# Multi-query attention on one core: a planner's times for GpSimd's loads, key copies and additions, and a fifth buffer for VectorE's weights

## The chip, the core and the metric

The kernel runs on one core of a Trainium2 chip. The metric is the device time of one execution in microseconds (us); below 2% two kernels of this case can hardly be told apart. TensorE (PE) multiplies matrices, VectorE (DVE), ScalarE (ACT) and GpSimd (POOL) work elementwise, SyncE (SP) issues DMAs. Each engine works through its own instructions in order, so a wait at the head holds all that is behind it.

## What is computed

Attention with 16 heads of queries and one head of keys and values, for 8 batches, 1024 positions and a head dimension of 64, float32 in and out:

```python
scores = np.matmul(q, k.transpose(0, 1, 3, 2)) / np.sqrt(head_dim)
weights = np.exp(scores - np.max(scores, axis=-1, keepdims=True))
weights = weights / np.sum(weights, axis=-1, keepdims=True)
attn_out = np.matmul(weights, v)
```

## The kernel before

**Tiles.** The work is 64 pairs of heads (8 batches by 8 pairs). A pair has 8 tiles of 128 keys, a tile two halves of 512 queries, so there are 1024 score tiles of 128 keys by 2 heads by 512 queries. A score is two matmuls of TensorE into one of three PSUM buffers (`score`, L574). It is then turned into weights, in one of two ways:

- ScalarE takes most scores: one exponential each (`exp_act`, L594), into `wt`, which has 20 buffers (ABUFS).
- VectorE takes a fifth of them, two tiles (four scores) at a time, called a duo, into `wd` with 4 buffers (DBUFS). It writes the scaled score as a 16-bit integer (`fixed`, L602), whose upper bits are already the exponent, and corrects it with a polynomial of the lower bits: `f` (L620), `m` (L623), `l` (L646, done by GpSimd in four parts), the product `m` (L631) and two products into `l` (L633). The correction is added to `wd` by a DMA that accumulates, issued from GpSimd (`add`, L658), two for each duo. In the first duo and the last two VectorE does `l` (L627) and the addition (L637) itself.

The weights are then multiplied with the values (`value`, L683: TensorE, 65 columns, of which the last sums the weights), seven blocks of 128 queries of a head at a time into one of two accumulators. VectorE takes the reciprocal of the sum (L692) and normalises into `osb` (L702), which holds the results of three pairs, and SyncE writes them out (L719). There are 8192 matmuls of L683 and 2048 of L574.

**Transfers.** Keys, values and queries are loaded by GpSimd's DMAs, which cast to float16. Queries come in groups of four pairs, in four parts (`load_part`, L503), with four buffers `qn`; SyncE issues for each part a DMA that transposes it into `qt` (`trans_q`, L512). Keys come batch by batch (`load_k`, L443); GpSimd copies one tile of them behind the others (`copy_k`, L457), and two transposing DMAs of SyncE make `k2t` (`trans_k`, L465). Transposes wait for the exponential before the last one planned and for the last addition (`after`); in the kernel before every addition waits for such an exponential too (L662).

**The order** on all five engines is written out by `plan`. It plays the work through with a cost for each step and emits the steps in order of its own time: the program then has that order, whatever the chip does. `transfers` gives for each load, key copy and transpose the progress in pairs at which it falls due. `issue` hands them to GpSimd and SyncE. In it an addition is ready ADD_0 + ADD_1 + ADD_L after its issue for TensorE (`ready`), transposes and additions are held apart by `hold`, a query load needs a free buffer (`free_q`), and a query transpose is planned LOAD_L after its load. A key copy has no such time: it is planned where it falls due, whether or not the load has landed. LEAD is how many pairs VectorE's scores may run ahead of ScalarE's. At each step TensorE takes a score for ScalarE, a score for VectorE or a block of values, by what the plan's model has ready.

Of the kernel before, what the change touches and what calls it, by code (L numbers as in the profile page):

```python
# [10 lines left out]
FP16 = mybir.dt.float16  # L11
# [6 lines left out]
P = 128  # L18
# [9 lines left out]
VEC_DEP = 0.12  # L28
POOL_S, POOL_F, POOL_L = 0.15, 1.05, 0.12
POOL_D = dict(add=1.0, loadq=0.85, loadk=0.85, copyk=0.95, loadv=1.2)  # L30
ADD_0, ADD_1, ADD_L = 2.0, 2.5, 3.5
TURN_0, TURN_1, LOAD_L = 1.0, 4.0, 6.0
NB, NG, OSB = 16, 7, 3
PITCH = 68
FIRST, DVE_0 = 4, 2.3
ABUFS, DBUFS = 20, 4
LAG, END = 1.0, 6.0
LEAD, LEAD_0, LEAD_END = 2.5, 1.5, 10.0
FIRST_Q, FIRST_G = 3.5, 22.0
QLEAD = 3.3  # L40
LATE = 2
# [4 lines left out]
FAR = 1e9  # L46
# [25 lines left out]
def transfers(NP):  # L72
    QP, HP = 4, 8
    res = []
    for g in range(1, NP // QP):
        for i in range(QP):
            at = QP * (g - 2) + i + 0.2 if g > 2 else 1.2 + 0.8 * i if g > 1 else 0.02 + 0.01 * i
            res += [(at, "loadq", g, i), (at + (0.5 if g > 1 else 0.0), "turnq", g, i)]
    for b in range(1, NP // HP):
        at = HP * (b - 1)  # L80
        res += [(at + 1.5, "loadk", b), (at + 2.2, "copyk", b), (at + 2.5, "turnk", b, 0),
                (at + 3.5, "turnk", b, 1), (at + 2.9, "loadv", b)]
    return sorted(res)


def plan(NP, NKT, stats=None):
# [3 lines left out]
    def emit(t, *op):  # L90
        ops.append((t, len(ops), op))

    def half(t):
# [4 lines left out]
        if i % 2 == 1:  # L98
            avail[d, i // 2] = pool + POOL_L

    def issue(t):
        nonlocal pool, sp, busy, hold, free_q
        while todo_d and todo_d[0][0] <= prog:
            x = todo_d.pop(0)[1:]
            (turns if x[0][:4] == "turn" else loads).append(x)
        if turns and t >= max(sp, busy - TURN_0):
            x = turns[0]
            at = landed.get(x[1:3] if x[0] == "turnq" else x[1:2], FAR)
            if at <= t:
                turns.pop(0)  # L110
                emit(t, *x)
                free_q += x[0] == "turnq"
                sp = t + TURN_0
                hold = t + TURN_1
        if pool > t or halves and zs:
            return
        if adds and adds[0][0] <= t and t >= hold - ADD_0:
            _, d, h = adds.pop(0)
            emit(t, "add", d, h)
            pool = t + POOL_D["add"]  # L120
            busy = max(busy, t + ADD_0) + ADD_1
            ready[duos[d][h]] = busy + ADD_L
        elif loads and not adds and (loads[0][0] != "loadq" or free_q > 0):
            x = loads.pop(0)
            free_q -= x[0] == "loadq"
            emit(t, *x)
            pool = t + POOL_D[x[0]]
            if x[0] in ("loadq", "copyk"):
                landed[x[1:]] = pool + (LOAD_L if x[0] == "loadq" else 0.0)

    pe = act = 0.0
    dve = DVE_0
# [22 lines left out]
    direct: set = set()  # L155
    pool = lock = sp = busy = hold = prog = 0.0
    todo_d = transfers(NP)
    free_q = 4
    adds: list = []
    loads: list = []  # L160
    turns: list = []
# [4 lines left out]
    while todo_g or groups:  # L166
        if pe <= dve:
            T = pe
            prog = ap + (na / nap if ap >= 0 else 0)
            issue(T)  # L170
            if not vunits and not over:
                lead = min(LEAD if prog > 4 else LEAD_0, LEAD * (NP - prog) / LEAD_END) if duos else 0
# [8 lines left out]
                if okay and prog < NP - STOP:  # L181
# [3 lines left out]
                    d = len(duos)  # L185
# [39 lines left out]
            for grp in groups:  # L225
                k, segs, left, a = grp
                for n, j in sorted(left):
                    gp, lo, hi = segs[n]
                    t = NKT * gp + j
                    if t in owner:  # L230
                        r = ready.get(t, FAR)
                    else:
                        r = max(
                            ready.get((t, c), FAR) for c in range(2)
                            if lo < NB // 2 + NB // 2 * c and hi > NB // 2 * c
                        )
                    if len(left) == NKT * len(segs):
                        r = max(r, acc[a])
# [6 lines left out]
            if av:  # L245
                x = pick[0][1][pick[1]]
                after = aa + AV_B * (x[2] - x[1]) + SWITCH
            if kind == "z":
                do = "qk"
            elif kind == "act":  # L250
                s = min(range(3), key=lambda s: slot[s])
                at = aq if slot[s] <= aq else slot[s] + WAKE
# [10 lines left out]
            if do == "qk":  # L263
                s = min(range(3), key=lambda s: slot[s])
                st = aq if slot[s] <= aq else slot[s] + WAKE
                pe, mode = st + QK_P, "qk"
                if kind == "z":
                    d, i = vunits.pop(0)
# [14 lines left out]
            elif do == "av":  # L283
                st = aa
# [10 lines left out]
                if not left:  # L295
                    acc[a] = FAR
                    r = pe - AV_B + PE_R
# [5 lines left out]
        else:  # L303
            T = dve
            issue(T)
            z = [x for x in zs if x[0] <= T]
            todo = [("ev", x) for x in evs if x[0] <= T and (
                x[4] == "rec" or x[:4] + ("rec",) not in evs)]
            if steps:
                x = steps[0]  # L310
# [6 lines left out]
            what, x = (free or todo or [("", None)])[0]  # L317
            if z:
                x = z[0]
# [15 lines left out]
            elif what == "ev":  # L335
                evs.remove(x)
                _, k, segs, a, kind = x
# [42 lines left out]
def kernel(  # L380
# [8 lines left out]
    B, S, H, D = q.shape  # L389
    assert D == 64 and S == 1024 and H % 4 == 0  # L390
    NKT = S // P
# [4 lines left out]
    QP = HP // 2  # L396
# [5 lines left out]
    consts = ctx.enter_context(tc.tile_pool(name="consts", bufs=1))  # L402
# [12 lines left out]
    osb = osbp.tile([P, OSB * NB, D], FP32, name="osb")  # L415
# [15 lines left out]
    def after(i, xs):  # L431
        for x in xs:
            tc.add_manual_dep(
                i.ins, x.ins.name,
                mybir.DependencyInfo(mybir.DependencyClass.Sync, mybir.DependencyReason.DATA),
                reason="transposes and additions apart",
            )
# [43 lines left out]
    def place_q(g):  # L481


        qt[g] = qtp.tile([P, QP * NKT + 1, P], FP16, tag="qt", name=f"qt{g}")[:, 0 : QP * NKT, :]
# [4 lines left out]
    def load_q(p):  # L489

        qn[0, p] = qp.tile([P, NKT, P], FP16, tag="qn", name=f"qn0_{p}")
        if p > 0:
            nc.gpsimd.dma_start(
                out=qn[0, p],
                in_=q[0, :, 2 * p : 2 * p + 2, :].rearrange("(c p) h d -> p c (h d)", p=P),
            )
# [29 lines left out]
    def load_first():  # L526

        st = kst.setdefault(0, {})
        st["kn"] = osb[:, 0:NKT, :]
        st["qf"] = osb[:, NB : 2 * NB, :].rearrange("p (c h) d -> p c (h d)", h=2)  # L530
        for c in range(NQC):
            x = slice(HT * c, HT * c + HT)
            nc.sync.dma_start(
                out=st["kn"][:, x, :], in_=k[0].rearrange("(p c) d -> p c d", p=P)[:, x, :])
            nc.scalar.dma_start(
                out=st["qf"][:, x, :],
                in_=q[0, :, 0:2, :].rearrange("(c p) h d -> p c (h d)", p=P)[:, x, :],
            )
        st["k16"] = consts.tile([P, NKT, 2, D], FP16, name="k160")
        st["k2t"] = kvp.tile([P, NKT + 1, P], FP16, tag="k2t", name="k2t0")[:, 0:NKT, :]  # L540
        place_q(0)
        load_q(0)
# [64 lines left out]
    def flat(x):  # L607
        return x.rearrange("p t h x -> p (t h x)")
# [44 lines left out]
            reason="VectorE reads PSUM next",  # L653
        )

    def add(d, h):
        x = slice(h * 2 * S, (h + 1) * 2 * S)
        added.append(nc.gpsimd.dma_start(  # L658
            out=flat(wd[d].bitcast(I16))[:, x], in_=tmp[d, "l"].bitcast(I16)[:, x],
            accum_op=ALU.add,  # L660
        ))
        after(added[-1], past[-2:-1])  # L662

    def value(k, seg, j, first, s):

# [28 lines left out]
    def normalise(k, segs):  # L694
# [14 lines left out]
        for p, lo, hi in segs:  # L709
# [8 lines left out]
            elif p < NP - 1 and left[p] == 0:  # L718
                nc.sync.dma_start(out=o, in_=x)  # L719

    ops, duos = plan(NP, NKT)
    ops = [op for _, _, op in ops]
    groups = grouped(NP)
    lasts = {}
    for op, *args in ops:
        if op == "av":
            lasts[args[0], args[1][0]] = args[2]
    load_first()
    load_q(1)
    load_v(0)  # L730
# [9 lines left out]
    with tc.manual_schedule(engines={ENG.PE, ENG.Activation, ENG.DVE, ENG.Pool, ENG.SP}):  # L740
# [4 lines left out]
        for op, *args in ops:  # L745
            if op == "qk":
# [3 lines left out]
                t, c, s = args  # L750
                if t in units:
                    d, i = units[t]
# [5 lines left out]
            elif op == "z":  # L758
                d, i = args
                fixed(duos[d][i // 2], i % 2)  # L760
            elif op == "step":
                poly(*args)
            elif op == "l":
                linear(*args)
            elif op == "add":
                add(*args)
            elif op == "av":
                value(*args)
            elif op == "rec":
                reciprocal(*args)  # L770
            elif op == "norm":
                normalise(*args)
            elif op == "loadq":
                load_part(*args)
            elif op == "turnq":
                trans_q(*args)
            elif op == "loadk":
                load_k(*args)
            elif op == "copyk":
                copy_k(*args)  # L780
            elif op == "turnk":
                trans_k(*args)
            elif op == "loadv":
                load_v(*args)
            else:
                raise ValueError(op)
# [28 lines left out]
```

## Time and profile before

| what | value |
|---|---|
| runs shown | 768.44, 773.98, 779.84 us; median 773.98 |
| profiled execution | 771.87 us, its span 770.0 us |
| mean granted clock of TensorE | 0.970 |
| busy in the span | ScalarE 746.5 us, VectorE 730.2, TensorE 686.7, GpSimd 394.4 |
| first and last exponential | start at 6.98 us, end at 758.82 us |
| additions, issue to landing | 6.7 us at the median, 102 of 512 KB |

In a row of groups, the numbers behind the first bar are the busy time in us and the mean duration of one in ns; behind the second bar is the idle time of the engine before them, with what ended it. A row of waits has the total in us, how often, and the longest. A row of the timeline has the start, the time that the row covers, the instruction, how many, and in brackets the idle time before it and what ended it. A row of sums by stretch of time has the busy time of TensorE's matmuls, of its weight loads, of VectorE, ScalarE and GpSimd with the number of instructions in brackets, then the granted clock of TensorE (1.00 is full), the busy share of the DMA engines and GB/s. TensorE's busy time is modelled at the ends of its matmuls.

### The profile page before, as it was taken

The numbers are of one execution on the slowest core, as the hardware profiler recorded it, in microseconds if no ns is written. First come the engines' busy times: TensorE is split into PE (matmuls) and PEld (weight loads), VectorE is DVE, ScalarE is ACT, GpSimd is POOL, SyncE is SP. The second block draws the span as 40 slices with busy tenths as digits, with TensorE's granted clock in tenths as the row PEclk, the third lists the DMA queues.
The fourth block names the chain that finished last, engine by engine and source line by source line (L and its number), as shares of the span: only waits on it lengthen the run. The fifth ranks groups of instructions, "written<-read, shape, count | busy, mean of one in ns | idle before, by whom it ended". The sixth has DMA issues, their size and how long they took to land.

```text
span 770.0 us, 23649 instructions
## 1 busy us (share of the span) xinstructions
PE 686.7 (89%) x10256; PEld 416.8 (54%) x10256; DVE 730.2 (95%) x815; ACT 746.5 (97%) x811; POOL 394.4 (51%) x405
## 2 busy tenths in 40 slices
PE   5888999998999799999989998979889998999985
PEld 2455565655555355555556555545555555556544
DVE  5999998999999879999999999989999999999997
ACT  7999999999999999999999999989999999999994
POOL 3256455555556544565656654655564646444410
PEclk8899999999999979999999999999999999999988
DMA  9789889998999997999989999999999998967443
GB/s 171 119 134 188 158 180 176 184 186 164 182 186 143 164 164 154 196 167 199 177 152 182 178 188 143 184 172 169 191 158 178 170 193 151 187 135 151 87 111 84
DMA packets 185624, 126.18 MB, mean 164 GB/s; under 512 B 89392, under 2 KB 172464, under 8 KB 185520
## 3 DMA queue, kind: packets, MB, share of 16 engines
q0 software_dynamic: 43456, 71.97, 57.0%
q1 hardware_dynamic: 140480, 51.92, 33.6%
q8 instruction: 80, 1.31, 0.7%
q10 hardware_dynamic: 1584, 0.79, 0.4%
q14 instruction: 24, 0.20, 0.1%
HBM read 37.75 MB, written 33.55 MB: 93 GB/s over the span
## 4 chain that ended last, share of the span: by engine, by line
ACT 62%; PE 12%; DVE 12%; issue 7%; DMA 6%; POOL 1%; POOLq 0%; DVEq 0%; ACTq 0%
ACT wt L594 61%; PE sc L574 6%; PE acc L683 5%; DMA wd<-l 4%; DVE wd L602 3%; DVE l L633 2%; DVE m L631 2%; DVE osb L702 1%; DVE m L623 1%; DMA k<-in_k_dram 1%; DVE f L620 1%; DMA k2t<-k 1%; POOL l L646 1%; DMA osb<-in_q_dram 0%; DVE wd L637 0%
## 5 line engine op out<-in xcount | busy, mean ns | idle before, releaser
L594 ACT ACTIVATE wt<-sc 128x1024 f16<-128x1024 f32 x808 | 744.0, 1196 | 8.5 <-PE sc L574 8.1
L574 PE MATMUL sc<-qt,k2t 64*128 64x512 f16 x2048 | 378.9, 392 | 66.7 <-ACT wt L594 52.0
L646 POOL TENSOR_SCALAR l<-f 128x1024 f16<-128x1024 uint16 x204 | 214.0, 1049 | 222.4 <-DVE m L631 111.4
L683 PE MATMUL acc<-v,wt 128*128 128x65 f16 x6464 | 316.9, 195 | 2.3 <-DVE osb L702 2.0
L683 PEld LDWEIGHTS <-wt 128*128 128x128 f16 x6464 | 239.5, 98 | 146.5 <-issue 145.3
L602 DVE TENSOR_SCALAR wd<-sc 128x1024 uint16<-128x1024 f32 x216 | 262.7, 1216 | 17.5 <-PE sc L574 16.6
L574 PEld LDWEIGHTS <-k2t 64*128 64x128 f16 x2048 | 123.3, 93 | 148.6 <-issue 98.9
L658 POOL DMA_DIRECT2D wd<-l x102 | 103.1, 1028 | 88.6 <-ACT wt L594 46.2
L633 DVE TENSOR_TENSOR l<-m,l 128x2048 int16<-128x2048 f16 x108 | 129.6, 1201 | 6.9 <-POOL l L646 6.6
L631 DVE TENSOR_TENSOR m<-f,m 128x4096 f16<-128x4096 uint16 x54 | 123.7, 2291 | 0.1
L683 PE MATMUL acc<-v,wd 128*128 128x65 f16 x1728 | 104.0, 195 | 3.8 <-DMA wd<-l 2.2
L683 PEld LDWEIGHTS <-wd 128*128 128x128 f16 x1728 | 71.7, 98 | 46.4 <-issue 40.2
L702 DVE TENSOR_TENSOR osb<-acc,rec 128x448 f32<-128x448 f32 (+4 forms) x165 | 91.0, 563 | 1.9 <-DVE rec L692 0.2
L623 DVE TENSOR_SCALAR m<-f 128x4096 f16<-128x4096 uint16 x54 | 69.4, 1285 | 0.3
L620 DVE TENSOR_SCALAR f<-wd 128x4096 uint16<-128x4096 uint16 x54 | 64.9, 1202 | 0.0
L503 POOL DMA_DIRECT2D qn<-in_q_dram x60 | 55.3, 922 | 18.7 <-DMA qt<-qn 8.5
L692 DVE RECIPROCAL rec<-acc 128x7 f32<-128x7 f32 (+1 forms) x147 | 27.9, 193 | 2.6 <-PE acc L683 2.2
L451 POOL DMA_DIRECT2D v<-in_v_dram x8 | 10.1, 1264 | 0.0
L457 POOL COPY k<-k 128x64 f16<-128x64 f16 x7 | 4.4, 635 | 8.6 <-DMA k<-in_k_dram 8.3
L637 DVE TENSOR_TENSOR wd<-wd,l 128x2048 uint16<-128x2048 uint16 x6 | 7.2, 1214 | 0.0
L443 POOL DMA_DIRECT2D k<-in_k_dram x7 | 5.7, 811 | 0.4
L560 PE MATMUL kps<-ident,k 128*128 128x128 f16 x8 | 1.2, 307 | 4.1 <-DVE k L548 4.1
(19 smaller groups left out, 19.4 us busy)
## 6 DMA issues: line engine op xcount, KB each, us to landing
wd<-l POOLq DMA_DIRECT2D x102, 512.0 KB, 6.7
out_dram<-osb SPq DMA_DIRECT2D x63, 512.0 KB, 6.2
qn<-in_q_dram POOLq DMA_DIRECT2D x63, 256.0 KB, 6.5
v<-in_v_dram POOLq DMA_DIRECT2D x8, 128.0 KB, 7.5
qt<-qn SPq DMA_TRANSPOSE x63, 4.2
k<-in_k_dram POOLq DMA_DIRECT2D x7, 128.0 KB, 6.8
osb<-in_q_dram ACTq DMA_DIRECT2D x2, 256.0 KB, 4.0
osb<-in_k_dram SPq DMA_DIRECT2D x2, 128.0 KB, 3.2
```

The lines of the kernel that those rows point to most:

```text
L503: nc.gpsimd.dma_start(out=qn[g, i], in_=q[b, :, 2 * QP * r : 2 * QP * (r + 1), :].rearrange("(c p) h d -> p c (h d)", p=P)[:, n * i : n * ...
L574: nc.tensor.matmul(sc[t, c][:, h, :].rearrange("p (i x) -> p i x", x=P), keys(p // HP, h, j), queries(p, c)[64 * h : 64 * h + 64, :, :], s ...
L594: past.append(nc.scalar.activation(out=wt[t][:, :, c * QC : (c + 1) * QC], in_=sc.pop((t, c)), func=EXP, scale=ascale))
L602: behind["dve"] = nc.vector.tensor_scalar(out=wt[t].bitcast(U16)[:, :, c * QC : (c + 1) * QC], in0=sc.pop((t, c)), scalar1=vscale, scalar2 ...
L620: i = V.tensor_scalar(out=new(d, "f", U16, 1), in0=z, scalar1=1023, scalar2=None, op0=ALU.bitwise_and)
L623: i = V.tensor_scalar(out=new(d, "m", FP16, 1), in0=tmp[d, "f"], scalar1=-ONE, scalar2=1.0 / ONE, op0=ALU.add, op1=ALU.mult)
L631: i = V.tensor_tensor(out=tmp[d, "m"], in0=tmp[d, "f"], in1=tmp[d, "m"], op=ALU.mult)
L633: i = V.tensor_tensor(out=tmp[d, "l"].bitcast(I16)[:, h], in0=tmp[d, "m"][:, h], in1=tmp[d, "l"][:, h], op=ALU.mult)
L646: n = nc.gpsimd.tensor_scalar(out=tmp[d, "l"][:, x], in0=tmp[d, "f"][:, x], scalar1=GB / ONE, scalar2=GA, op0=ALU.mult, op1=ALU.add,)
L658: added.append(nc.gpsimd.dma_start(out=flat(wd[d].bitcast(I16))[:, x], in_=tmp[d, "l"].bitcast(I16)[:, x], accum_op=ALU.add,))
L683: nc.tensor.matmul(acc[k][:, n + x - lo, 0 : D + 1], w[:, h, i * P : (i + 1) * P], kst[p // HP]["v"][:, j, 0 : D + 1], start=first and x = ...
L702: behind["dve"] = nc.vector.tensor_tensor(out=osb[:, x % (OSB * NB) : x % (OSB * NB) + m, :], in0=a[:, n : n + m, 0:D], in1=r[:, n : n + m ...
```

## The change

Constants of the plan: an addition is planned as ready 2.7 + 2.2 + 8.0 after its issue instead of 2.0 + 2.5 + 3.5; a load lands after 8.0 instead of 6.0; a query buffer counts as free 8.0 after its transpose is issued (TURN_L, new) instead of at once; VectorE's weights get a fifth buffer, and its scores may run 3.0 pairs ahead instead of 2.5. Query loads fall due somewhat earlier, their transposes 0.7 instead of 0.5 of a pair later. A key copy is planned only once its load has landed by that time, and the transpose of keys only after the copy. An addition waits for an exponential only if the plan held it back for a transpose. The float16 copy of the first batch's keys lies in the third part of `osb` instead of in a tile of its own. The diff, cut to its core:

```diff
-ADD_0, ADD_1, ADD_L = 2.0, 2.5, 3.5
-TURN_0, TURN_1, LOAD_L = 1.0, 4.0, 6.0
+ADD_0, ADD_1, ADD_L = 2.7, 2.2, 8.0
+TURN_0, TURN_1, TURN_L, LOAD_L = 1.0, 4.0, 8.0, 8.0
...
-ABUFS, DBUFS = 20, 4
+ABUFS, DBUFS = 20, 5
...
-LEAD, LEAD_0, LEAD_END = 2.5, 1.5, 10.0
+LEAD, LEAD_0, LEAD_END = 3.0, 1.5, 10.0
...
-            at = QP * (g - 2) + i + 0.2 if g > 2 else 1.2 + 0.8 * i if g > 1 else 0.02 + 0.01 * i
-            res += [(at, "loadq", g, i), (at + (0.5 if g > 1 else 0.0), "turnq", g, i)]
+            at = QP * (g - 2) + 0.85 * i - 0.6 if g > 2 else 1.2 + 0.7 * i if g > 1 else 0.02 + 0.01 * i
+            res += [(at, "loadq", g, i), (at + (0.7 if g > 1 else 0.0), "turnq", g, i)]
...
+    def can(x, t):
+        if x[0] == "loadq":
+            return bool(freed) and freed[0] <= t
+        return x[0] != "copyk" or landed["loadk", x[1]] <= t
...
-            at = landed.get(x[1:3] if x[0] == "turnq" else x[1:2], FAR)
+            at = landed.get(x[1:3] if x[0] == "turnq" else ("copyk", x[1]), FAR)
...
-                free_q += x[0] == "turnq"
+                if x[0] == "turnq":
+                    freed.append(t + TURN_L)
...
-            _, d, h = adds.pop(0)
-            emit(t, "add", d, h)
+            at, d, h = adds.pop(0)
+            emit(t, "add", d, h, at < hold - ADD_0)
...
-        elif loads and not adds and (loads[0][0] != "loadq" or free_q > 0):
+        elif loads and not adds and can(loads[0], t):
             x = loads.pop(0)
-            free_q -= x[0] == "loadq"
+            if x[0] == "loadq":
+                freed.pop(0)
...
-            if x[0] in ("loadq", "copyk"):
-                landed[x[1:]] = pool + (LOAD_L if x[0] == "loadq" else 0.0)
+            landed[x[1:] if x[0] == "loadq" else x] = pool + (LOAD_L if x[0] != "copyk" else 0.5)
...
-        st["k16"] = consts.tile([P, NKT, 2, D], FP16, name="k160")
+        st["k16"] = osb[:, 2 * NB : 2 * NB + NKT, :].bitcast(FP16).rearrange("p c (r d) -> p c r d", r=2)
...
-    def add(d, h):
+    def add(d, h, held):
...
-        after(added[-1], past[-2:-1])
+        if held:
+            after(added[-1], past[-2:-1])
```

More of the change, by code (lines that the diff above doesn't have):

```diff
@@ L99, in half @@
             avail[d, i // 2] = pool + POOL_L
+    def can(x, t):
+        if x[0] == "loadq":
+            return bool(freed) and freed[0] <= t
+        return x[0] != "copyk" or landed["loadk", x[1]] <= t
     def issue(t):
-        nonlocal pool, sp, busy, hold, free_q
+        nonlocal pool, sp, busy, hold
         while todo_d and todo_d[0][0] <= prog:
@@ L157, in plan @@
     todo_d = transfers(NP)
-    free_q = 4
+    freed = [0.0] * 4
     adds: list = []
```

## The prediction

> **What bounds the kernel now.** I read the busy table first, then the groups of instructions with their idle time, the chain of waits, the sums by stretch of time for the granted clock, and the timeline around each gap of ScalarE.
>
> ```profile
> PE 686.7 (89%) x10256; PEld 416.8 (54%) x10256; DVE 730.2 (95%) x815; ACT 746.5 (97%) x811; POOL 394.4 (51%) x405
> L594 ACT ACTIVATE wt<-sc 128x1024 f16<-128x1024 f32 x808 | 744.0, 1196 | 8.5 <-PE sc L574 8.1
> L646 POOL TENSOR_SCALAR l<-f 128x1024 f16<-128x1024 uint16 x204 | 214.0, 1049 | 222.4 <-DVE m L631 111.4
> ACT wt L594 <- PE sc L574: 8.1, 17, 1.6
> ```
>
> ScalarE is the bound: 808 exponentials at 744.0/808 = 0.92 us each, with only 8.5 us idle among them. Every wait ended when TensorE had delivered a score late. What the change can win is therefore in those gaps and in the ends of the span; GpSimd's 222 us of idle time cost nothing by themselves. The largest cluster of gaps:
>
> ```profile
> 502.03 1.20 POOL L443 DMA_DIRECT2D k<-in_k_dram  x1
> 503.31 1.03 POOL L646 TENSOR_SCALAR l<-f 128x1024 f16<-128x1024 uint16 x1
> 510.62 0.24 POOL L457 COPY k<-k 128x64 f16<-128x64 f16 x1 [6.28 <-DMA k<-in_k_dram]
> 513.96 1.23 DVE L633 TENSOR_TENSOR l<-m,l 128x2048 int16<-128x2048 f16 x1 [3.36 <-POOL l L646]
> 515.78 0.37 PE L683 MATMUL acc<-v,wt 128*128 128x65 f16 x7 [1.32 <-DVE osb L702]
> 516.72 1.02 ACT L594 ACTIVATE wt<-sc 128x1024 f16<-128x1024 f32 x1 [0.88 <-PE sc L574]
> 519.35 1.02 ACT L594 ACTIVATE wt<-sc 128x1024 f16<-128x1024 f32 x1 [1.60 <-PE sc L574]
> 520.72 2.12 ACT L594 ACTIVATE wt<-sc 128x1024 f16<-128x1024 f32 x2 [0.35 <-PE sc L574]
> 523.07 5.61 ACT L594 ACTIVATE wt<-sc 128x1024 f16<-128x1024 f32 x6 [0.23 <-PE sc L574]
> ```
>
> Here GpSimd's key copy stands in its queue right behind the load that it needs; the next polynomial part `l` is behind the copy, VectorE's product waits for `l`, the normalisation behind it holds an accumulator, TensorE waits for that, and ScalarE runs dry: 0.88 + 1.60 + 0.35 + 0.23 = 3.06 us. The second kind of gap has another cause:
>
> ```profile
> 260.00:265.00 5.00, 3.31 (x35) 1.54 (x34) 4.91 (x6) 5.00 (x7) 3.88 (x4) 1.00 0.32 66
> 265.00:270.00 5.00, 2.95 (x12) 0.62 (x11) 2.32 (x2) 5.00 (x7) 3.77 (x5) 0.62 1.05 195
> 270.00:275.00 5.00, 4.31 (x24) 1.31 (x22) 3.46 (x6) 5.00 (x6) 3.10 (x3) 0.50 0.93 138
> 65.00:70.00 5.00, 3.18 (x24) 1.16 (x23) 5.00 (x4) 5.00 (x7) 1.55 (x3) 1.00 0.91 150
> 263.46 0.39 PE L574 MATMUL sc<-qt,k2t 64*128 64x512 f16 x2 [0.52 <-ACT wt L594]
> 277.61 2.12 ACT L594 ACTIVATE wt<-sc 128x1024 f16<-128x1024 f32 x2 [0.38 <-PE sc L574]
> 280.25 5.61 ACT L594 ACTIVATE wt<-sc 128x1024 f16<-128x1024 f32 x6 [0.51 <-PE sc L574]
> 720.64 4.87 ACT L594 ACTIVATE wt<-sc 128x1024 f16<-128x1024 f32 x5 [0.37 <-PE sc L574]
> 743.12 3.96 ACT L594 ACTIVATE wt<-sc 128x1024 f16<-128x1024 f32 x4 [0.19 <-PE sc L574]
> 747.31 1.02 ACT L594 ACTIVATE wt<-sc 128x1024 f16<-128x1024 f32 x1 [0.24 <-PE sc L574]
> 748.51 2.92 ACT L594 ACTIVATE wt<-sc 128x1024 f16<-128x1024 f32 x3 [0.18 <-PE sc L574]
> 740.00:745.00 5.00, 4.21 (x33) 1.71 (x30) 4.69 (x8) 4.81 (x7) 0.00 (x0) 0.56 0.18 48
> ```
>
> (The column behind POOL is the granted clock.) From 262 us on the plan gives TensorE scores alone; it does a pair in 0.39 us and idles 0.52. Its clock then falls to one half, and when the value matmuls come back they are too slow: ScalarE waits. I call this a fall of the clock. The same happens at 717 and 741. But 65 to 70 us, hardly denser, keeps 1.00, so a short thin stretch falls only sometimes.
>
> **The change part by part.** Both built programs have the same instructions of each kind on each engine (808 exponentials, 54 pairs of tiles for VectorE, 102 additions); only order and waits differ. So nothing is won in busy time.
>
> *Key copies, loads.* Counted in exponentials of the program's order, the distance from a key load to its copy was 2 to 19 and is now 11 to 19. Eleven are 10.1 us, and the load of the cluster above took 8.6 us (502.03 to 510.62) to let the copy go, so that wait goes, with all its four gaps. A single exponential takes 1.02 us instead of 0.92, so each gap costs another 0.1: the term is -3.5 us.
>
> ```profile
> POOL k L457 <- DMA k<-in_k_dram: 8.3, 3, 6.3
> POOL qn L503 <- DMA qt<-qn: 8.5, 2, 7.4
> POOL wd L658 <- ACT wt L594: 46.2, 40, 2.7
> DMA to landing us min/median/max: 4.5/6.7/11.3
> 179.55 0.24 PE L683 MATMUL acc<-v,wd 128*128 128x65 f16 x2 [0.73 <-DMA wd<-l]
> 180.42 3.77 ACT L594 ACTIVATE wt<-sc 128x1024 f16<-128x1024 f32 x4 [0.42 <-PE sc L574]
> 447.10 0.73 PE L574 MATMUL sc<-qt,k2t 64*128 64x512 f16 x3 [0.19 <-DMA k2t<-k]
> ```
>
> The query loads' 8.5 us on GpSimd have no gap of ScalarE behind them: 0. Late copies bring late transposes: from the last key transpose to its first score there are at least 10 exponentials, before and after, as from the last query transpose at least 9. In this trace the distance of 10 ended in the 0.19 us above, so I take 0, between 0 and 1 us.
>
> *Additions ready later* (ADD_L). From an addition to the first value matmul on its tile it is at least 14 exponentials (12.9 us) instead of 9 (8.3 us). The row with min/median/max is the additions' landing, 11.3 us at most: that was not covered and now is. The gap at 180.42 goes: -0.5 us with its restart.
>
> *Waits of the additions.* 20 of 102 wait for an exponential instead of 99. That frees GpSimd from most of the 46.2 us in 40 pauses, which hide behind its idle time: 0. Additions leave earlier and can run beside transposes; a landing would have to pass 12.9 us to be seen.
>
> *Fifth buffer, LEAD, the keys' first tile moved into `osb`.* The casts are as many as before, and that third of `osb` gets its first result only with pair 2, when they have long been read: 0. The buffer and LEAD let VectorE's scores run further ahead; they show in TensorE's order.
>
> *The end.*
>
> ```profile
> 759.87 1.09 PE L683 MATMUL acc<-v,wt 128*128 128x65 f16 x30 [0.67 <-DVE osb L702]
> 762.13 0.66 PE L683 MATMUL acc<-v,wd 128*128 128x65 f16 x16 [1.18 <-DVE wd L637]
> 763.27 0.66 PE L683 MATMUL acc<-v,wd 128*128 128x65 f16 x16 [0.47 <-DVE wd L637]
> ```
>
> After the last exponential TensorE waits 2.3 us for VectorE. VectorE's last score tile now has 17 exponentials behind it instead of 9, 7.3 us more, so its last tile is ready in time. The last normalisations still follow the last exponential: between 0 and -2.3, I take -1.2 us.
>
> *What the new order costs TensorE.* I count stretches in which any five scores in a row carry at most 14 value matmuls (40 is the mean), after the first 50 us, which are alike. Before has 9, one of them ten scores or longer (the one at 262 us). The new order has 25, seven of them that long (by the place in the order at about 52, 72, 253, 345, 428, 538 and 699 us). In this trace the long one and 2 of the 8 short ones made the clock fall. By that rate: 7 + 18 x 2/8 = 11.5 falls instead of 3. A fall cost 0.38 + 0.51, 0.37, and 0.19 + 0.24 + 0.18 us, with 0.1 for each gap 1.09, 0.47 and 0.91: 0.82 on average. Term: 8.5 x 0.82 = +7.0 us. Its ends: nothing, if VectorE's and TensorE's reserves cover it, and 1.7 us a fall (the longest gap above, 1.60, with its restart), because the stretches now alternate with fuller ones: up to 230 value matmuls in 16 scores, where it was 180. I take the mean, as it comes from three falls of this kernel.
>
> The Trainium skill, "TensorE: Matmul & The Clock Gate", section "HAM oscillation — how this bites in real kernels", asks only that there be no idle gaps of TensorE over about 3.4 us. This trace differs: the clock went to 0.50 with pauses of 0.52 us. By the page this term would be nothing; that case is the first rival.
>
> **Sum** against the profiled execution (771.87 us, of which 770.0 are span): 771.87 - 3.5 - 0.5 - 1.2 + 7.0 = 773.7 us. The median of the runs shown is 2.1 us above that execution. I add nothing for it: waits such as the one at 510 us, which vary with the DMAs, are what the change takes out.
>
> **The rivals.**
>
> *The thin stretches are free.* For it: 65 to 70 us above. Against it: 262 us. 771.87 - 5.2 = 766.7 us; 764.2 if the three falls of before go too, 763.1 with all of the end.
>
> *The thin stretches are the new bound (slower).* A fall is followed by a full stretch at half clock, where TensorE has no reserve. With 16 falls (the long ones and half of the short) at 1.7 us: 16 x 1.7 - 2.5 - 5.2 = +19.5, so 791.4 us. At 16 falls it is slower by 2% from 1.58 us a fall on. Against it: 0.82 measured, and ScalarE has up to three score buffers in hand.
>
> *The change doesn't do what it says.* Additions beside transposes make DMAs slower, and GpSimd goes on waiting for a key load, or TensorE for an addition: the 3.5 us stay, some 777 us. For it: landings from 4.5 to 11.3 us for one size. Against it: the distances above.
>
> **How the numbers follow.** The sum has 0.55, the free stretches 0.25, the new bound 0.10, the last rival 0.10. The first has its own range from 769 (8.5 falls more at 0.3 us) to 781 (11.5 falls at 1.45 us). The range of 763 to 784 takes in the free stretches and leaves out the new bound and the outer part of the first. About 2% is what a measurement of this kernel can tell from no change (its own runs go from 768.44 to 779.84). Faster by 2% is below 758.5 us, under every case worked out: 0.02. Slower by 2% is over 789.5 us, most of the new bound: 0.07. Within: 0.91.
>
> **What would show it.** Right: no wait of L457 for its load, no 3 us wait of VectorE for `l`, no wait of TensorE for `wd`; half clock near 52, 72, 253, 345, 428, 538 and 699 us, each with gaps of ScalarE of 0.4 to 1 us behind it. Wrong: a clock at 1.00 in those places (then 764 to 767 us), gaps of over 1.5 us at each (then 790 us), or ScalarE waiting where TensorE waits for `qt` or `k2t`.

## The result, and the profile after

| | median | runs | ratio to before, 95% interval |
|---|---|---|---|
| before | 774.77 us | 768.44 to 779.84 (6) | |
| after | 765.35 us | 763.29 to 768.90 (6) | 0.988 [0.983, 0.993] |

The change makes the kernel 1.2% faster: the interval doesn't reach 1, but the gain is below 2%. Ratios and intervals, here and below, leave out the few runs over 1.5% above the fastest of the same kernel, medians do not. The time lies inside the stated range (763 to 784 us), but beside the likeliest value of 773.7: the nearest case was the first rival, thin stretches that are free (766.7 us). It will turn out that this was not the reason. The profiled execution took 765.40 us, its span 763.7 (before 771.87 and 770.0), so 6.3 us of span are to be explained. First the page and the rows of waits after the change (L600 is the exponential, L580 the score, L509 the query load, L664 the addition):

```profile
PE 679.2 (89%) x10256; PEld 409.1 (54%) x10256; DVE 728.7 (95%) x815; ACT 746.1 (98%) x811; POOL 400.4 (52%) x405
L600 ACT ACTIVATE wt<-sc 128x1024 f16<-128x1024 f32 x808 | 743.6, 1181 | 7.6 <-PE sc L580 7.2
...
POOL qn L509 <- DMA qt<-qn: 15.7, 3, 7.3
POOL wd L664 <- ACT wt L600: 28.1, 11, 3.3
```

ScalarE's busy time is the same to 0.4 us, and its idle time among the exponentials has hardly changed: 7.6 us instead of 8.5. GpSimd waits for no key load and TensorE for no addition any more. The query loads' wait for transposes is 15.7 us instead of 8.5, but with their other waits they stand 18.7 us in both profiles. So the gaps have moved rather than gone. The timeline of ScalarE after the change, its eight places with gaps after the first 50 us:

```profile
79.87 2.12 ACT L600 ACTIVATE wt<-sc 128x1024 f16<-128x1024 f32 x2 [0.67 <-PE sc L580]
260.22 1.94 ACT L600 ACTIVATE wt<-sc 128x1024 f16<-128x1024 f32 x2 [0.22 <-PE sc L580]
262.51 3.07 ACT L600 ACTIVATE wt<-sc 128x1024 f16<-128x1024 f32 x3 [0.35 <-PE sc L580]
430.12 2.12 ACT L600 ACTIVATE wt<-sc 128x1024 f16<-128x1024 f32 x2 [0.38 <-PE sc L580]
432.80 2.85 ACT L600 ACTIVATE wt<-sc 128x1024 f16<-128x1024 f32 x3 [0.56 <-PE sc L580]
510.20 2.08 ACT L600 ACTIVATE wt<-sc 128x1024 f16<-128x1024 f32 x2 [0.29 <-PE sc L580]
541.78 1.94 ACT L600 ACTIVATE wt<-sc 128x1024 f16<-128x1024 f32 x2 [0.78 <-PE sc L580]
674.75 1.94 ACT L600 ACTIVATE wt<-sc 128x1024 f16<-128x1024 f32 x2 [0.78 <-PE sc L580]
705.52 1.02 ACT L600 ACTIVATE wt<-sc 128x1024 f16<-128x1024 f32 x1 [0.23 <-PE sc L580]
706.71 1.94 ACT L600 ACTIVATE wt<-sc 128x1024 f16<-128x1024 f32 x2 [0.17 <-PE sc L580]
738.39 1.02 ACT L600 ACTIVATE wt<-sc 128x1024 f16<-128x1024 f32 x1 [0.35 <-PE sc L580]
739.91 1.94 ACT L600 ACTIVATE wt<-sc 128x1024 f16<-128x1024 f32 x2 [0.50 <-PE sc L580]
748.98 8.45 ACT L600 ACTIVATE wt<-sc 128x1024 f16<-128x1024 f32 x9
```

These gaps add up to 5.28 us, with 0.1 for each of the 12 restarts 6.5 us. The sums by stretch of time, for two of these places (the clock stands behind GpSimd's column), show the clock at about one half:

```profile
420.00:425.00 5.00, 3.62 (x53) 1.99 (x52) 4.76 (x5) 5.00 (x7) 2.38 (x2) 1.00 0.41 82
425.00:430.00 5.00, 4.47 (x28) 1.60 (x27) 5.00 (x7) 4.73 (x6) 4.22 (x6) 0.56 1.06 190
535.00:540.00 5.00, 3.91 (x23) 1.29 (x23) 4.58 (x8) 5.00 (x7) 3.56 (x4) 0.50 1.05 148
```

The last row of the timeline is the other half of the story. The last exponential ends at 748.98 + 8.45 = 757.43 us, only 1.4 us earlier than before (758.82). From there to the end it was 11.14 us and is now 6.25 us: **4.9 of the 6.3 us were won behind the last exponential.** ScalarE's last exponentials and VectorE's last rows, three lines from before and two from after the change:

```profile
748.51 10.31 ACT L594 ACTIVATE wt<-sc 128x1024 f16<-128x1024 f32 x11 [0.18 <-PE sc L574]
760.86 2.35 DVE L637 TENSOR_TENSOR wd<-wd,l 128x2048 uint16<-128x2048 uint16 x2
763.66 0.20 DVE L692 RECIPROCAL rec<-acc 128x6 f32<-128x6 f32 x1 [0.45 <-PE acc L683]
754.42 2.35 DVE L643 TENSOR_TENSOR wd<-wd,l 128x2048 uint16<-128x2048 uint16 x2
757.58 0.20 DVE L699 RECIPROCAL rec<-acc 128x6 f32<-128x6 f32 x1 [0.81 <-PE acc L690]
```

After the change VectorE's last tile is ready at 756.8 us, before the last exponential ends, and the first of the last three normalisations begins 0.15 us behind it (757.58). Before the change the tile was ready at 763.21 us, and the normalisation began at 763.66 us, 4.8 us behind the last exponential.

**Theory of the end:** what the change won is where the plan puts VectorE's last duo; in the middle, the key load's wait that went (-3.5 us) is offset by new falls of the clock. **Rival:** GpSimd's waits on DMAs were the cost, as the change's title has it, or the fifth buffer is needed for what was won. A second question was the price of the falls.

### The profile page after: what moved, and what is told of

Its sections match the earlier page's. It is cut to its first block, busy times and chain, and to the rows that moved or that the text cites. A ratio compares the mean times of both kernels' runs of the same rounds, so it can differ in the third digit from the quotient of the medians.

```text
span 763.7 us, 23613 instructions
## 1 busy us (share of the span) xinstructions
PE 679.2 (89%) x10256; PEld 409.1 (54%) x10256; DVE 728.7 (95%) x815; ACT 746.1 (98%) x811; POOL 400.4 (52%) x405
## 4 chain that ended last, share of the span: by engine, by line
ACT 70%; PE 13%; issue 8%; DVE 8%; DMA 0%; DVEq 0%; ACTq 0%
ACT wt L600 70%; PE sc L580 7%; PE acc L690 6%; DVE wd L608 3%; DVE l L639 1%; DVE osb L709 1%; DVE m L637 1%; DVE m L629 1%; DVE f L626 1%; DMA osb<-in_q_dram 0%; DVE rec L699 0%; ACT qn L556 0%; PE qps L570 0%; ACT qt L572 0%; PE kps L566 0%
## 5 line engine op out<-in xcount | busy, mean ns | idle before, releaser
L600 ACT ACTIVATE wt<-sc 128x1024 f16<-128x1024 f32 x808 | 743.6, 1181 | 7.6 <-PE sc L580 7.2
L580 PE MATMUL sc<-qt,k2t 64*128 64x512 f16 x2048 | 379.0, 395 | 72.9 <-ACT wt L600 61.5
L690 PE MATMUL acc<-v,wt 128*128 128x65 f16 x6464 | 309.5, 196 | 1.5 <-issue 0.7
L580 PEld LDWEIGHTS <-k2t 64*128 64x128 f16 x2048 | 117.0, 94 | 170.7 <-issue 124.0
L664 POOL DMA_DIRECT2D wd<-l x102 | 110.6, 1114 | 91.7 <-DVE l L639 29.5
L509 POOL DMA_DIRECT2D qn<-in_q_dram x60 | 53.8, 898 | 18.7 <-DMA qt<-qn 15.7
L457 POOL DMA_DIRECT2D v<-in_v_dram x8 | 8.1, 1010 | 0.0
L463 POOL COPY k<-k 128x64 f16<-128x64 f16 x7 | 6.7, 959 | 0.4
```

What stands on the lines that cost most here:

```text
L509: nc.gpsimd.dma_start(out=qn[g, i], in_=q[b, :, 2 * QP * r : 2 * QP * (r + 1), :].rearrange("(c p) h d -> p c (h d)", p=P)[:, n * i : n * ...
L580: nc.tensor.matmul(sc[t, c][:, h, :].rearrange("p (i x) -> p i x", x=P), keys(p // HP, h, j), queries(p, c)[64 * h : 64 * h + 64, :, :], s ...
L600: past.append(nc.scalar.activation(out=wt[t][:, :, c * QC : (c + 1) * QC], in_=sc.pop((t, c)), func=EXP, scale=ascale))
L664: added.append(nc.gpsimd.dma_start(out=flat(wd[d].bitcast(I16))[:, x], in_=tmp[d, "l"].bitcast(I16)[:, x], accum_op=ALU.add,))
L690: nc.tensor.matmul(acc[k][:, n + x - lo, 0 : D + 1], w[:, h, i * P : (i + 1) * P], kst[p // HP]["v"][:, j, 0 : D + 1], start=first and x = ...
```

## The experiments

Each ran with the kernel before on the same chip, whose median was 772.87 us in the first four, 771.64 in the next four and 773.23 in the last four. Ratios are to these.

**1 to 4: the parts of the change.** The first has the transfers alone. Against the changed kernel:

```diff
-ADD_0, ADD_1, ADD_L = 2.7, 2.2, 8.0
+ADD_0, ADD_1, ADD_L = 2.0, 2.5, 3.5
-ABUFS, DBUFS = 20, 5
+ABUFS, DBUFS = 20, 4
-LEAD, LEAD_0, LEAD_END = 3.0, 1.5, 10.0
+LEAD, LEAD_0, LEAD_END = 2.5, 1.5, 10.0
...
-        if held:
-            after(added[-1], past[-2:-1])
+        after(added[-1], past[-2:-1])
```

> The kernel before with the change's transfers alone (due times of loads and transposes, key copies after their loads, TURN_L, LOAD_L); four buffers, LEAD 2.5, the old times of additions and their waits. VectorE's last score has 9 exponentials behind it, as before; one long thin stretch near 66 us. Theory of the end (what was won is mostly that VectorE's last tile is ready earlier): about 771 us, 3.5 us less than before at most, since the wait for the key load goes, and the stretch from the last exponential to the end stays near 11 us. Rival (GpSimd's waits on DMAs are the gain): 765 to 767 us, as the changed kernel.

Measured: 776.56 us, 1.004 [1.001, 1.008]: slower than before, and than the 771 us expected. GpSimd waits for no key load, and the end takes 10.9 us, as the theory says. But a new wait came, which I had not expected. TensorE and ScalarE in this run:

```profile
454.94 0.60 PE L580 MATMUL sc<-qt,k2t 64*128 64x512 f16 x1 [4.26 <-DMA k2t<-k]
456.52 1.02 ACT L600 ACTIVATE wt<-sc 128x1024 f16<-128x1024 f32 x1 [6.58 <-PE sc L580]
```

Copies that are planned later make the transposes behind them later. In this order one key transpose stands 6 exponentials (5.5 us) ahead of its first score, where it is at least 10 in the kernels before and after. ScalarE's other large gap of this run, 3.96 us at 86.86 us, stands behind the long thin stretch; experiment 4 has one like it.

The second has the fifth buffer with its LEAD alone. Against the kernel before:

```diff
-ABUFS, DBUFS = 20, 4
+ABUFS, DBUFS = 20, 5
-LEAD, LEAD_0, LEAD_END = 2.5, 1.5, 10.0
+LEAD, LEAD_0, LEAD_END = 3.0, 1.5, 10.0
...
-        st["k16"] = consts.tile([P, NKT, 2, D], FP16, name="k160")
+        st["k16"] = osb[:, 2 * NB : 2 * NB + NKT, :].bitcast(FP16).rearrange("p c (r d) -> p c r d", r=2)
```

> The kernel before with the fifth buffer, LEAD 3.0 and the keys' tile in osb alone. VectorE's last score has 18 exponentials behind it, there is no long thin stretch, and the distances from key load to copy are 3 at the least, so GpSimd still waits for key loads. Theory of the end: 768 to 770 us, with 6 to 7 us from the last exponential to the end. Rival (GpSimd's waits are the gain): 774 us, no change.

Measured: 762.93 us, 0.987 [0.984, 0.991]: all that the whole change wins. The end takes 6.1 us, and between the first 50 us and the last exponential no fall of the clock is left. The time is below the 768 to 770 us expected, since the last exponential ends earlier too, at 754.51 us. GpSimd's and ScalarE's waits, and the way from one key copy to a gap:

```profile
POOL k L457 <- DMA k<-in_k_dram: 7.0, 2, 3.7
L594 ACT ACTIVATE wt<-sc 128x1024 f16<-128x1024 f32 x808 | 742.7, 1206 | 5.6 <-PE sc L574 5.4
596.59 0.23 POOL L457 COPY k<-k 128x64 f16<-128x64 f16 x1 [3.67 <-DMA k<-in_k_dram]
599.11 1.23 DVE L633 TENSOR_TENSOR l<-m,l 128x2048 int16<-128x2048 f16 x1 [1.11 <-POOL l L646]
604.45 0.39 PE L574 MATMUL sc<-qt,k2t 64*128 64x512 f16 x2 [0.63 <-DVE wd L602]
605.55 2.86 ACT L594 ACTIVATE wt<-sc 128x1024 f16<-128x1024 f32 x3 [0.35 <-PE sc L574]
```

GpSimd still waits 7.0 us for key loads, until 418 and 597 us. Behind the second VectorE waits 1.11 us for `l` and works without a pause from there on, its next score buffer comes free late, TensorE waits 0.63 us for it, and ScalarE has a gap of 0.35 us; behind the first there is one of 0.26 us, 17 us later, whose cause was not followed. So such a wait, here 3.67 us, cost a small part of what the one of 6.28 us at 510 us in the kernel before cost with its four gaps (3.06 us).

The third is the changed kernel with DBUFS 4 and LEAD 2.5.

> The changed kernel with four buffers and LEAD 2.5 again. VectorE's last score has 7 exponentials behind it; GpSimd's waits on key loads stay away. Theory of the end: 770 to 773 us, with 11 to 13 us from the last exponential to the end. Rival: 765 to 767 us.

Measured: 780.62 us, 1.010 [1.006, 1.014], above the 770 to 773 us expected. The end takes 15.5 us, more than expected for 7 exponentials; and TensorE waits 4.0 us for a key transpose until 449 us, which was not expected either.

The fourth is the changed kernel with `ADD_0, ADD_1, ADD_L = 2.0, 2.5, 3.5`.

> The changed kernel with the old times of additions (2.0, 2.5, 3.5). VectorE's last score has 19 exponentials behind it. Thin stretches are 10 instead of 25, additions are 9 exponentials ahead of their use instead of 14. If a fall of the clock costs 0.84 us: 2 to 4 falls instead of 8, 761 to 763 us, less up to 1 us for TensorE's waits on additions. If thin stretches cost nothing: 765 us, or a little more for the waits on additions.

Measured: 765.68 us, 0.991 [0.988, 0.994], with four falls after the first 50 us. The expectation of 761 to 763 missed, and the number is the one expected if thin stretches cost nothing (765); the trace shows that they did cost. One of the few thin stretches left is 20 scores long, and more was lost behind it than behind a fall elsewhere. Two sums by stretch of time, TensorE and ScalarE there, and TensorE at another gap:

```profile
70.00:75.00 5.00, 3.51 (x14) 0.79 (x14) 4.91 (x5) 5.00 (x7) 4.33 (x5) 0.50 0.44 90
80.00:85.00 5.00, 3.44 (x46) 2.37 (x45) 4.66 (x8) 3.05 (x4) 4.56 (x4) 0.50 1.09 164
83.30 2.49 PE L690 MATMUL acc<-v,wt 128*128 128x65 f16 x42 [1.42 <-DVE osb L709]
87.11 3.77 ACT L600 ACTIVATE wt<-sc 128x1024 f16<-128x1024 f32 x4 [4.07 <-PE sc L580]
171.15 0.29 PE L690 MATMUL acc<-v,wd 128*128 128x65 f16 x4 [1.52 <-DMA wd<-l]
```

Behind the thin stretch TensorE first waits 1.42 us for a normalisation; then the value matmuls that were put off come in one block, at half clock, and no score gets between them until 86.54 us. So the 4.07 us are not the fall's alone. At 171 us TensorE waits for an addition again, and ScalarE has a gap of 1.17 us: the later times of additions had taken such a wait away.

**5 and 6: the end by itself.** The fifth is the kernel before with one constant changed, four buffers and all:

```diff
-            at = QP * (g - 2) + i + 0.2 if g > 2 else 1.2 + 0.8 * i if g > 1 else 0.02 + 0.01 * i
+            at = QP * (g - 2) + i + 0.0 if g > 2 else 1.2 + 0.8 * i if g > 1 else 0.02 + 0.01 * i
```

> The kernel before with one constant changed: query loads fall due 0.2 of a pair earlier. Four buffers, the old times of additions, the old waits, key loads 6 exponentials ahead of their copies at the least. By its own working the plan then leaves 18 exponentials behind VectorE's last score instead of 9, and the long thin stretch at 264 us is gone. Theory of the end (what counts is where the plan happens to put the last tiles and the thin stretches, whatever moved them): 764 to 768 us, with 6 us from the last exponential to the end. Rival (the fifth buffer itself is needed): 773 us, no change.

Measured: 759.59 us, 0.984 [0.980, 0.988], with 6.0 us behind the last exponential and one fall after the first 50 us. That is below the 764 to 768 us expected: the last exponential ends at 752.44 us too, 6.4 us earlier than before, with 1.1 us of gaps behind the first 50 us where there were 6.2. The fifth buffer isn't needed for what the change won: 0.2 of a pair in the loads' due times leads the plan to the better end as well. The sixth holds back the last duo in the changed kernel:

```diff
-                if okay and prog < NP - STOP:
+                if okay and prog < NP - STOP and (len(duos) < 53 or prog >= 62.7):
```

> The changed kernel with VectorE's last duo held back until 62.7 pairs, so that 8 exponentials are behind its last score instead of 17; all before it is as in the changed kernel. Theory of the end: the stretch from the last exponential to the end grows from 6 to 11 or 12 us, 770 to 772 us. Rival (what was won lies in the middle): 765 to 766 us.

Measured: 770.24 us, 0.998 [0.995, 1.001], where the changed kernel had 0.988 [0.983, 0.993]. ScalarE's last exponentials and VectorE's last rows:

```profile
734.15 19.70 ACT L600 ACTIVATE wt<-sc 128x1024 f16<-128x1024 f32 x21
756.01 2.35 DVE L643 TENSOR_TENSOR wd<-wd,l 128x2048 uint16<-128x2048 uint16 x2
758.97 0.20 DVE L699 RECIPROCAL rec<-acc 128x6 f32<-128x6 f32 x1 [0.61 <-PE acc L690]
```

The last exponential ends at 753.85, the normalisations wait for VectorE's tile until 758.97, and the end (765.1) is 11.3 us behind the last exponential, 5.0 more than in the changed kernel. The profiled execution is only 1.4 us longer than the changed kernel's, because its last exponential ended 3.6 us earlier: it had 2.3 us of gaps after the first 50 us instead of 5.6, although the order is the same up to the last 30 scores. Both runs went as the theory of the end said, and against its rival. In all 14 profiles the stretch behind the last exponential goes with the exponentials planned behind VectorE's last score: 5.8 to 6.3 us with 17 to 19 of them, 10.9 to 11.3 with 8 or 9, 15.5 with 7.

**7 and 9: the price of the falls.** In the seventh, TensorE does eight small matmuls into unused columns of an open accumulator behind each of 90 scores.

```diff
+    def keep_busy(k):
+        for _ in range(8):
+            nc.tensor.matmul(
+                spare[k], ident, ident[:, 0:32], start=False, stop=False, skip_group_check=True)
...
+                if scores - 1 in thin and open_:
+                    keep_busy(min(open_))
```

> The changed kernel with 720 small matmuls more, eight behind each of the 90 scores in thin stretches, into unused columns of an accumulator that nothing reads, so that TensorE stays busy there. If a fall of the clock costs 0.84 us and comes from the thin stretch: one or two falls instead of nine, and 758 to 761 us. If falls cost nothing, or ScalarE's gaps there have another cause: 765 us, or more for the added work.

Measured: 763.77 us, 0.989 [0.985, 0.994]: between the 758 to 761 and the 765 us expected, so inconclusive. Where no accumulator was open nothing was added, which left 86 of the 176 scores in thin stretches without them; five falls stayed where the changed kernel has eight, and ScalarE's gaps moved. The ninth reaches all thin stretches (176 scores, L580):

```diff
-        for h in range(2):
+        for h in (0, 1) * (2 if len(sc_made) in thin else 1):
```

> The changed kernel with 176 scores, those in thin stretches, computed twice into the same buffer, one directly behind the other; the result is the same. TensorE is then busy for about 0.6 of 0.92 us instead of 0.4 there, in all thin stretches and not only in those with an open accumulator, as in the run with small matmuls. If a fall of the clock costs 0.84 us: at most two falls in place of nine, and 758 to 761 us. If falls cost nothing, or the gaps come from the full stretches behind the thin ones: 765 us, with the gaps in their places although the clock stays at 1.00.

Measured: 762.23 us, 0.989 [0.984, 0.995], again between the two values expected. In the profiled execution (760.81 us, span 759.1) no fall is left between the first 20 us and the last exponential. The same stretches as above, and ScalarE over the two places at 430 us:

```profile
420.00:425.00 5.00, 4.14 (x54) 2.18 (x52) 4.55 (x5) 5.00 (x7) 2.80 (x2) 1.00 0.52 101
425.00:430.00 5.00, 4.60 (x60) 2.17 (x56) 5.00 (x7) 5.00 (x6) 3.81 (x5) 1.00 1.04 186
425.28 10.38 ACT L613 ACTIVATE wt<-sc 128x1024 f16<-128x1024 f32 x11
```

The gaps of 0.38 and 0.56 us are gone with the fall, and the span is 4.6 us shorter than the changed kernel's. So the falls do cost time, in the profiled executions. How much is open: experiment 6's execution, with the changed kernel's order and six falls, had its last exponential only 1.0 us later than this one. The mean granted clock of the six runs was 0.987 to 0.999, of the changed kernel's six 0.955 to 0.971. Still the medians don't tell the two kernels apart (0.989 against 0.988): two of the six runs of this one were at 769 and 771 us, with clocks of 0.987 and 0.993, and what lengthened them is not known.

**8: the key load's wait alone.** The kernel before with `loadk` due at +1.0 instead of +1.5; the rest of the order is as before.

> The kernel before with key loads due half a pair earlier, so that they are 14 exponentials or more ahead of their copies instead of 2; the rest of the order, the end with 9 exponentials among it, is as before. GpSimd does not wait for key loads. Theory of the end: 770 to 773 us, 0 to 3.5 us won with the cluster at 510 us. Rival (GpSimd's waits on DMAs are the gain): 765 to 767 us.

Measured: 767.52 us, 0.995 [0.992, 0.999]. The end takes 10.9 us, as before, GpSimd waits for no key load, and about 0.5% is won, 4.1 us between the medians where 0 to 3.5 were expected. In its profiled execution another wait stands where that one was gone: TensorE waits 4.84 us for an addition until 459.60 us. The falls that before had at 717 and 741 us are not in it, although the orders of TensorE, ScalarE and VectorE are the same.

**10: the additions' waits.** The changed kernel with `if held:` taken away.

> The changed kernel with all 102 additions waiting for an exponential again, instead of 20. My prediction took these waits at nothing: 764 to 767 us, as the changed kernel, with GpSimd idle some 20 to 40 us more before its additions. Rival (GpSimd's freedom is part of the gain): 767 us or more.

Measured: 767.99 us, 0.995 [0.992, 0.998]. GpSimd's row, and ScalarE behind a fall that the changed kernel's profile does not have; then the same stretch of time in the changed kernel's profile and in experiment 6's, and ScalarE there in experiment 6:

```profile
POOL wd L664 <- ACT wt L600: 72.8, 52, 4.8
...
351.79 1.02 ACT L600 ACTIVATE wt<-sc 128x1024 f16<-128x1024 f32 x1 [0.39 <-PE sc L580]
353.26 1.02 ACT L600 ACTIVATE wt<-sc 128x1024 f16<-128x1024 f32 x1 [0.46 <-PE sc L580]
354.68 1.02 ACT L600 ACTIVATE wt<-sc 128x1024 f16<-128x1024 f32 x1 [0.39 <-PE sc L580]
356.15 2.85 ACT L600 ACTIVATE wt<-sc 128x1024 f16<-128x1024 f32 x3 [0.45 <-PE sc L580]
...
345.00:350.00 5.00, 4.23 (x55) 2.45 (x53) 5.00 (x9) 5.00 (x7) 3.40 (x4) 1.00 1.07 207
345.00:350.00 5.00, 4.98 (x63) 2.69 (x63) 5.00 (x9) 4.99 (x6) 2.21 (x3) 0.72 1.08 207
339.21 21.57 ACT L600 ACTIVATE wt<-sc 128x1024 f16<-128x1024 f32 x23
```

The waits are back, 72.8 us instead of 28.1, and the time is the one that the rival gave (767 us or more), perhaps 0.6% longer; the two intervals, [0.992, 0.998] and [0.983, 0.993], touch. The profile has falls at 58, 185 and 349 us that the changed kernel's has not. They need no cause in GpSimd's pauses: experiment 6's execution, with the changed kernel's waits and up to there its order, has falls at 58, 184 and 344 us. Which thin stretches fall thus differs between executions of one order, and so does the price: behind its falls at 58 and 344 us experiment 6 has no gap of ScalarE, behind the one at 349 us this run has 2.1 us with the restarts.

**11 and 12: two kernels built on this.** The eleventh is the kernel before with query loads due 0.4 of a pair earlier (`+ i - 0.2`) and key copies at +2.3.

> The kernel before with two due times changed: query loads 0.4 of a pair earlier, key copies 0.1 later. Four buffers. 17 exponentials behind VectorE's last score, 5 thin stretches (one of 13 scores at 65 us), key loads 10 exponentials ahead of their copies at the least. Theory of the end and of key waits: 757 to 761 us. If the change's buffers or the times of additions matter by themselves: 765 us or more.

Measured: 764.49 us, 0.989 [0.984, 0.994], with five runs from 757.84 to 766.70 and one of 774.35; the 757 to 761 us expected were missed. Its profiled execution was the shortest of all (757.84 us, ScalarE idle 2.1 us), but it did not hold that, and what the others lost is not known. The twelfth is the fifth with 60 scores twice.

> The kernel before with query loads 0.2 of a pair earlier (759.6 us in its run) and 60 scores in thin stretches computed twice. If a fall of the clock costs its gaps: the fall at 36 us and its gaps of 1.4 us go, 757 to 759 us. If not: 759 to 760 us.

Measured: 759.34 us, 0.984 [0.980, 0.988], as the fifth. The fall at 36 us and its gaps went, and the span (759.6, with the last exponential at 753.63 instead of 752.44) is still longer than the fifth's (758.4): TensorE waits for additions in seven places, and ScalarE has a gap of 1.30 us at 642 us. What such a fall is worth in this kernel isn't shown.

## Why the prediction was right in range and beside the mark in its sum

- *ScalarE is the bound, nothing is won in busy time*: right (743.6 against 744.0 us).
- *Key copies, -3.5 us*: the wait and the four gaps are gone. By itself it is worth 0.5% (experiment 8). Experiment 2 adds that such a wait can cost much less: 0.35 us behind one of 3.67 us.
- *Late transposes, 0*: right for this change, for which the distances were read; experiment 1 shows the wait for `k2t` that was named as a sign of being wrong, at a distance of 6.
- *Additions ready later, -0.5 us*: right; TensorE waits for no addition after the change, and with the old times it does again (experiment 4, 1.52 us at 171 us).
- *Waits of the additions, 0*: open, between 0 and some 0.6% in favour of the change.
- *The end, -1.2 us, at most -2.3*: **this is the step that failed.** It measured -4.9. I summed the time that TensorE sat idle behind VectorE, but work that it did between those waits was late as well: it was queued behind them. The bound was to be had from the trace: from the last exponential (758.82) to the first of the last normalisations (763.66) it was 4.8 us. Experiment 6, which changes the end alone, brings the 11.3 us back, 5.0 more than in the changed kernel.
- *Thin stretches, +7.0 us from 11.5 falls at 0.82*: the falls came, with gaps behind them, but the count was too high. There are 8 falls between the first 50 us and the last exponential, where 3 were counted before (the kernel before has a fourth, at 519 us, in the cluster that the term of the key copies covers). Of the seven long stretches named five fell (those at 72, 253, 428, 538 and 699 us) and two kept the clock (52 and 345 us); of the 18 short ones three fell. With 0.81 us for each the term is 6.5 - 2.5 = +4.0. That 0.81 meets the 0.82 of the prediction is in part luck: with the same order experiment 6 has six falls at about 0.5 us, among them those at 52 and 345 us and not those at 72 and 253 us. "The thin stretches are free", the rival whose time came out, isn't what the traces show: in experiment 9 gaps went with the falls, and its span is 4.6 us shorter; its median doesn't show it.

The two terms that were off, the end by 3.7 us and the falls by 3.0, were off the same way. The range held because it took in the 766.7 us of that rival; that the time came out near it is luck.

With the measured terms the sum is 771.87 - 3.5 - 0.5 - 4.9 + 4.0 = 767.0; measured are 765.40. Gaps of before at 40, 248 and 479 us that are smaller or gone after the change, 0.8 us in all, make up part of the rest. The median moved further (9.4 us) than the profiled execution (6.5): that of before was one of its faster ones, and here I had added nothing.

The Trainium skill's rule on idle gaps ("TensorE: Matmul & The Clock Gate", section "HAM oscillation — how this bites in real kernels": none over about 3.4 us) has not been what decides here: in the 6.8 us ahead of each of the eight falls TensorE was never idle for more than 0.53 us at a time. Behind 3.62 of 5 us busy (420 to 425 us) the clock fell, with 4.14 in experiment 9 it stayed; but with 3.50 of 5 at 340 to 345 us of the changed kernel's profile it stayed as well, so the busy time of such a stretch doesn't decide alone.

## What to carry to other kernels

Where a planner writes out the order, a small change of a cost or a due time gives another order as a whole; look first at what that did at the end of the program and in the thinnest stretches, and only then at the wait that the change was made for. At the end, price a late engine from the last item of the bounding engine to the first final step, not by the idle time of the engine in between. The transfers and the times of additions won nothing here on top of the fifth buffer and its LEAD, and one due time in the old plan (experiment 5) did no worse than all of it, as far as the intervals tell (0.984 [0.980, 0.988] against 0.988 [0.983, 0.993]).

## What the runs showed of the hardware that was not expected

- TensorE's clock went to one half with TensorE never idle for more than 0.53 us at a time in the 6.8 us ahead; computing scores twice, with no other change to the order, kept it at 1.00 in the profiled execution between the first 20 us and the last exponential.
- With one and the same order of TensorE up to there the falls come at different places from one execution to the next: the stretch near 345 us kept the clock in the changed kernel's profile and lost it in those of experiments 6 and 10.
- The cost of a fall varies, with one order too: nothing (58 and 344 us in experiment 6), 0.4 to 1.1 us in the changed kernel's profile, 2.1 us at 349 us in experiment 10. The 4.07 us of experiment 4, where a thin stretch of 20 scores was followed by its value matmuls in one block, hold a wait of 1.42 us for a normalisation.
